# Other durations in the planner's table of a two-block transformer kernel on one core

## The chip, the cores and the metric

The kernel runs on one core of a Trainium2 chip. The metric is the device time of one execution in microseconds. A core has TensorE (PE, matrix products, with the loading of weights shown apart as PEld), VectorE (DVE), ScalarE (ACT), GpSimd (POOL) and SyncE (SP), which issues the loads. Every engine works through its own queue in order, and a semaphore makes an instruction wait for one on another engine.

## The reference

Two layers of a decoder block and then one block with a mixture of experts, for 256 tokens of 1024 features, all in float32.

```python
def first_block(x, mem, ...):
    h = x
    for l in range(DEPTH):                      # DEPTH = 2
        mix = hybrid_mixer(h, ...)              # recurrence and windowed attention, gated
        h = layer_norm(DEEPNORM_ALPHA * h + mix, ln1_g[l], ln1_b[l])
        h = layer_norm(DEEPNORM_ALPHA * h + cross_attention(h, mem, ...), ln2_g[l], ln2_b[l])
        h = layer_norm(DEEPNORM_ALPHA * h + swiglu(h, ffn_wi[l], ffn_wo[l]), ln3_g[l], ln3_b[l])
    return h
```

The second block modulates its input by vectors that come from a condition (`silu(cond) @ w + b`), attends to a neighbourhood on a grid and to a context, adds a gated spatial unit, and sends every token to two of four experts in one of four groups (16 experts, 512 hidden features each).

## The kernel before

*Products.* Weights come from memory in units of 128 x 1024 elements (512 KB). Each unit is split into two rounded parts: ACT writes `hi` (L425, in `_prep`), DVE writes `lo` = unit - `hi` (L426). A product is three matmuls, hi*hi, hi*lo and lo*hi (`mm3`, L540 to L542). With the weights stationary (`feat_block`) a unit is 24 matmuls of 256 columns, with the tokens stationary (`token_block`) it is 12 of 512 columns for the two token tiles of 128 tokens. Six pairs of `hi` and `lo` tiles exist, and a few units are split ahead (`prepare`, L489).

*Streams.* The work is written as generators ("streams"): parts of the recurrence, attention groups (`swa_group`, L957), norms (`layer_norm`, L662), products, and so on. A stream emits some instructions and yields the engines whose work it waits for, or a condition. `Streams.run` (L208) holds a list of streams in order of priority and decides which one goes on. It serves main streams and, behind them, fill streams that use the gaps. Products that can always run stand last, so they fill the time in which the chains of small steps wait.

*The planner.* `Net.record` (L289) runs the whole body once without emitting anything. In that dry run a `Clock` (L37) takes the place of the chip: `Clock.cost` (L75) gives the duration of each instruction, `Clock.issue` (L95) puts it on its engine's queue behind what it needs, with `HOP` for the way from one engine to another. The order found is kept as a script and the real run repeats it. Three decisions hang on the clock:

- In `Streams.run`, `clock.now` is the planned front of PE. The first stream in the list whose due time has passed goes on (L240); if none is due, the one that is due first (L238). After a step its due time is the end of the engines that it named, plus `HOP` (L256).
- In `Net.step` (L429) an additional weight split is planned when the dry run's vector and scalar engines both stand more than 1.0 us behind `clock.now` (L434).
- In `Net.weight` (L462) the products for the modulation's vectors (`ada`, L1311, its DVE products at L1328) advance by one unit, after at least 2 weight units if the planned vector engine stands behind `clock.now`, after 16 in any case (L476).

Where a unit is loaded to (`lender`, L399) follows from the order and from how many tiles are in use at each step of it.

The steps named below: in `layer_norm` the sum with the residual (L672, DVE), the square (L676, ACT, with a bias and a sum), small DVE steps (L680 to L686), the power on GpSimd (L687) and the last product (L691, DVE); transposes by PE (`flip`, L649); in `modulated` the scaling of the rows ahead of the transposes (L1372, ACT); in `router` (L1655) a copy of the shift (L1663, DVE) and eight products with it (L1667, PE); in `swa_group` the exponentials (L988, ACT); in `cross_q` a copy out of a bank (L1086, ACT), which the transposes behind it read.

Of the kernel before, what the change touches and what calls it, by code (L numbers as in the profile page):

```python
# [27 lines left out]
# columns of w_in  # L28
# [3 lines left out]
def f(ap):  # L32
    """The float32 pattern of an operand that was rounded for the tensor engine."""
    return ap.bitcast(F)


class Clock:  # L37
    """Stands for the chip in a dry run: what instructions take, each engine in its order, each after what it needs."""

    BASE, ROW, CELL, HOP = 1 << 40, 1 << 16, 128, 0.15  # L40
# [34 lines left out]
    def cost(engine, op, out, ins, accum):  # L75
        size = lambda a: int(np.prod([d[1] for d in tuple(a.ap)[1:]]))
        n = max([size(a) for a in [out] + ins if a is not None] or [1])
        if engine == "tensor":
            rhs = ins[1] if len(ins) > 1 else out
            n = size(rhs)  # L80
            if op == "transpose":
                return 2 * 128 / 2400.0
            part = tuple(out.ap)[0][1] / 128.0 if tuple(out.ap)[0][1] < 64 else 1.0
            slow = 4 if rhs.dtype != R or n < 256 else 1
            return max(part * n * slow / 2400.0, size(ins[0]) * (4 if rhs.dtype != R else 1) / 2400.0) + 0.0027
        if op == "dma_start":
            return n * 512 / 360e3
        if engine == "scalar":
            return 0.13 + n / 1300.0 + (0.09 if accum else 0.0)
# [3 lines left out]
        return 0.3 + 0.16 * n if op == "tensor_tensor" else 0.1  # L93

    def issue(self, engine, op, args, kw):  # L95
# [14 lines left out]
        hop = lambda w: w[0] + (self.HOP if w[1] != who else 0.0 if who == "tensor" else 0.06)  # L110
# [19 lines left out]
    def peak(self, tag, n):  # L130
        """How many tiles of that tag are in use at once, by the number of units taken."""
        count = [0] * (n + 1)
        for kind, first, last in self.lives.values():
            if kind == tag:
                for i in range(first, min(last, n) + 1):
                    count[i] += 1
        return count
# [16 lines left out]
class Shelf:  # L154
    """Tiles of a dry run."""
# [8 lines left out]
class Marks(dict):  # L164
    """What is there, and since when."""
# [19 lines left out]
class Late:  # L185
    """A stream that may go on in the next run."""
# [5 lines left out]
class Streams:  # L192
    """Runs several generators that emit instructions, in order of priority.

    A generator yields the engines whose work it waits for; a function is yielded to wait for its truth.
    The order is found in a dry run, by the clock, and repeated from script.
    """

# [9 lines left out]
    def run(self, main, fill=()):  # L208
        """Runs main to its end but for the streams in it that are Late; fill serves the gaps; what is left has to end the next time."""
# [54 lines left out]
class Net:  # L264
# [24 lines left out]
    def record(self, body, lend=True):  # L289
        """A dry run of body, for the order of its instructions and of its weights; then it can run."""  # L290
# [16 lines left out]
    def lasting(self, *tiles):  # L307
        """Tiles that are of use after the dry run's body."""
# [41 lines left out]
    def prepare_const(self):  # L350
        nc, c = self.nc, self.const
        # softplus(-lambda) of both layers, then its multiples
# [33 lines left out]
    def _consumed(self, back):  # L386
        """The raw unit is of no more use."""
# [7 lines left out]
    def _free(self, i):  # L395
        """The units before unit i that are not kept are of no more use."""
        self.splits = set(j for j in self.splits if j >= i or j in self.held)

    def lender(self):  # L399
        """Where the next unit may be loaded to; tiles are lent as long as none will be short of them."""  # L400
# [28 lines left out]
    def step(self):  # L429
        """After each step of a stream."""  # L430
# [20 lines left out]
    def keep(self, n):  # L451
        """Waits until n more units may be kept."""
# [4 lines left out]
    def drop(self, i):  # L457
        """Unit i has been kept and is of no more use."""
# [3 lines left out]
    def weight(self, src, cols=512, raw=False, kept=None):  # L462
        """The next unit, [128, 1024 / cols, cols]: (hi, lo), or as it is; kept: takes its number until it is dropped."""
# [25 lines left out]
    def prepare(self, i, taken=False):  # L489
        """Splits ahead of unit i, as far as the units held allow; taken: not that unit itself."""  # L490
# [12 lines left out]
    def _dry_prepare(self, i, end, taken):  # L503
        """What follows is not known yet and taken for units to be split."""
# [39 lines left out]
    def feat_block(self, x, src):  # L544
        """[feature, token] product: W stationary; src(k): unit of input chunks 2k and 2k + 1, x = (hi, lo) [128, 8, 256]."""
# [16 lines left out]
    def token_block(self, x, src, done=None, tmajor=False, ready=None):  # L562
        """[token, feature] product: x() stationary; done(t, bank) when a token tile is through; ready(t, q): x is there."""
# [44 lines left out]
    def split(self, hi, lo, src):  # L608
        """hi + lo = src exactly, each with the tensor engine's mantissa."""
# [36 lines left out]
    def flip(self, b, src, n=4):  # L646
        """Transposes n [128, 128] blocks of src into a bank."""
# [10 lines left out]
    def bcast(self, row_ap, n):  # L658
        """A DRAM row on every partition."""
        return bass.AP(tensor=row_ap.tensor, offset=row_ap.offset, ap=[[0, 128]] + list(row_ap.ap)[-n:])  # L660

    def layer_norm(self, t, h, res, gb, hn, after):  # L662
        """hn()[:, t] = LN(alpha h + res) with g, b; then after(t). The squares are taken about the mean of the first half."""
# [15 lines left out]
        # minus the mean; how far it is from the first half's  # L679
# [15 lines left out]
    def transposes(self, t, new):  # L695
        """The new h of token tile t transposed, as (hi, lo)."""
# [12 lines left out]
    def norms(self, l, i, h, res, new, after, early):  # L709
        """The streams that take the sums res into new["hn"] and after it; new[t]: that token tile is through."""  # L710
# [26 lines left out]
    def gelu2(self, out, x):  # L737
        """out = 2 gelu(x) for a bank x."""
# [8 lines left out]
    def rnn_conv(self, l, hT, st):  # L747
        """xc (feature, token) and its rounded parts."""
# [21 lines left out]
    def rnn_gates(self, l, st):  # L770
        """tanh of half the recurrence gate's and the input gate's argument."""
# [24 lines left out]
    def rnn_scan(self, l, st):  # L796
        """y = h gelu(gr) as (hi, lo)."""
# [5 lines left out]
        for k in range(8):  # L803
            # u = tanh(-log_a / 2)
# [5 lines left out]
        for h in range(2):  # L810
            i = (slice(None), slice(4 * h, 4 * h + 4), slice(None))
            s = self.k4().rearrange("p (k c) -> p k c", c=256)
            # a = (1 - u) / (1 + u), from the exponential by one correction
# [8 lines left out]
            # b = sqrt(1 - a^2) i xc, sqrt(1 - a^2) = sqrt(u) (1 + a)  # L822
# [39 lines left out]
    def tanh_gate(self, l, hT, col, st, name, wait=None):  # L862
        """tanh of half the gate's argument."""
# [22 lines left out]
    def swa_q(self, l, hT, st, n, ready=None):  # L886
        """Half the heads of q, scaled, rotated and transposed."""
# [29 lines left out]
    def swa_kv(self, l, hT, st):  # L917
        """k and v of both token tiles in a bank; then k, each head twice, rotated and transposed with zeros for the other half."""
# [38 lines left out]
    def swa_group(self, l, g, st):  # L957
        """Attention over the window with sinks, four heads."""
# [66 lines left out]
    def branches(self, l, st):  # L1025
        """(feature, token) sum of the gated branches as (hi, lo)."""
# [26 lines left out]
    def residual(self, x, w, res, ready=None, tmajor=(False, True)):  # L1053
        """x() @ w by token: banks res[n, t]."""
# [7 lines left out]
    def cross_k(self, l, c, st, away=False):  # L1062
        """Keys of the memory, two heads; away: out to the memory."""
# [16 lines left out]
    def cross_q(self, l, hT, st, old):  # L1080
        """Two heads by token, then two by feature."""
# [24 lines left out]
    def cross_heads(self, l, hp, st):  # L1106
        """Attention over the memory, two heads: (feature, token) as (hi, lo)."""
# [45 lines left out]
    def ffn(self, l, hT, res, old, first):  # L1153
        """The gated product: banks res[n, t]."""
# [61 lines left out]
    def first_hidden(self, t, first):  # L1216
        """The first hidden features of a token tile, found by token."""
# [1034 lines left out]
```

## Time and profile before

| | |
|---|---|
| median of 3 runs | 1573.4 us (1572.85 to 1573.48) |
| span of the profiled execution | 1570.5 us |
| PE busy | 1519.7 us (97%), 9434 instructions |
| DVE busy | 1183.8 us (75%) |
| ACT busy | 907.3 us (58%) |
| GpSimd busy | 42.1 us (3%) |
| read from memory | 339.71 MB, 218 GB/s over the span |

Busy time is the union of an engine's instructions. Matmuls are pipelined, so a record is longer than the distance between two starts; the distance is what PE needs for one. The granted clock is TensorE's, as a share of 2.4 GHz.

### The profile page before, as it was taken

To read this page: it belongs to the slowest core of one execution; us is meant where nothing else is said; L and a number is where in the kernel's file an instruction comes from. 1 tells how busy PE (TensorE), PEld (TensorE's weight loads), DVE (VectorE), ACT (ScalarE), POOL (GpSimd) and SP (SyncE) were. 2 spreads that over 40 slices of the span, in tenths; PEclk is the share of its full clock that TensorE was granted. 3 is DMA by queue.
4 is the path that set the end of the run, shared out by engine and by line. 5 is a ranking of instruction groups with operands and counts; after the bars stand their busy time and mean duration, and the time that the engine had idled before them with its cause. 6 is when DMAs were issued, how large, how long until landed. Compare 5 with 4: busy or idle time off the path is not lost. (4 is left out here: it accounts for less than half of the span.)

```text
span 1570.5 us, 24658 instructions
## 1 busy us (share of the span) xinstructions
PE 1519.7 (97%) x9434; PEld 1349.3 (86%) x9434; DVE 1183.8 (75%) x1715; ACT 907.3 (58%) x1350; POOL 42.1 (3%) x48
## 2 busy tenths in 40 slices
PE   8999999999999999999999999999899999999997
PEld 7998999887999979988988779999687778888886
DVE  6968877467887668778877577766675678999996
ACT  6687544444444445775556544444555568787774
POOL 0000000000000010000000000000020000000000
PEclk9999999999999999999999999999899989999999
DMA  9545647558766555346575487765463539999972
GB/s 350 165 136 177 238 150 270 188 185 287 244 217 209 183 201 161 114 156 208 195 282 179 128 297 244 240 205 165 138 235 121 162 130 316 391 375 391 380 280 82
DMA packets 188476, 344.55 MB, mean 219 GB/s; under 512 B 12352, under 2 KB 67520, under 8 KB 187456
## 3 DMA queue, kind: packets, MB, share of 16 engines
q1 hardware_dynamic: 187328, 339.76, 63.1%
q0 software_dynamic: 1024, 3.15, 0.6%
q8 instruction: 76, 1.25, 0.3%
q14 instruction: 48, 0.39, 0.1%
HBM read 339.71 MB, written 3.15 MB: 218 GB/s over the span
## 5 line engine op out<-in xcount | busy, mean ns | idle before, releaser
L540 PE MATMUL bank<-act,hi 128*128 128x256 f32 x1664 | 476.7, 286 | 0.0
L542 PE MATMUL bank<-act,lo 128*128 128x256 f32 x1664 | 470.8, 283 | 0.0
L541 PE MATMUL bank<-act,hi 128*128 128x256 f32 x1664 | 470.7, 283 | 0.0
L426 DVE TENSOR_TENSOR lo<-raw,hi 128x1024 fp32r<-128x1024 f32 x220 | 264.6, 1221 | 94.2 <-ACT hi L425 89.2
L540 PEld LDWEIGHTS bank<-act,hi 128*128 128x128 f32 x1664 | 319.0, 192 | 5.2 <-issue 3.6
L541 PEld LDWEIGHTS bank<-act,hi 128*128 128x128 f32 x1664 | 319.1, 192 | 2.1 <-issue 1.0
L542 PEld LDWEIGHTS bank<-act,lo 128*128 128x128 f32 x1664 | 318.9, 192 | 0.0
L540 PE MATMUL bank<-hi,act 128*128 128x512 f32 (+1 forms) x752 | 301.2, 401 | 7.9 <-ACT hi L425 6.2
L426 DVE TENSOR_TENSOR lo<-act,hi 128x1024 fp32r<-128x1024 f32 x222 | 264.2, 1221 | 50.6 <-ACT hi L425 49.3
L541 PE MATMUL bank<-lo,act 128*128 128x512 f32 (+1 forms) x752 | 294.0, 391 | 0.5 <-DVE lo L426 0.5
L542 PE MATMUL bank<-hi,act 128*128 128x512 f32 (+1 forms) x752 | 293.8, 391 | 0.0
L425 ACT ACTIVATE hi<-raw 128x1024 fp32r<-128x1024 f32 x220 | 228.5, 1055 | 103.4 <-PE bank L541 39.7
L425 ACT ACTIVATE hi<-act 128x1024 fp32r<-128x1024 f32 x222 | 227.8, 1054 | 78.6 <-PE bank L541 39.7
L426 DVE TENSOR_TENSOR lo<-k,hi 128x1024 fp32r<-128x1024 f32 x122 | 146.1, 1221 | 40.8 <-ACT hi L425 35.4
L540 PEld LDWEIGHTS bank<-hi,act 128*128 128x128 f32 x752 | 144.0, 192 | 37.7 <-ACT hi L425 7.9
L542 PEld LDWEIGHTS bank<-hi,act 128*128 128x128 f32 x752 | 144.0, 191 | 31.3 <-DVE act L611 1.5
L541 PEld LDWEIGHTS bank<-lo,act 128*128 128x128 f32 x752 | 144.4, 192 | 28.1 <-DVE lo L426 1.0
L425 ACT ACTIVATE hi<-k 128x1024 fp32r<-128x1024 f32 x122 | 126.5, 1055 | 37.8 <-PE bank L541 19.8
L540 PE MATMUL bank<-hi,k 128*128 128x512 f32 (+1 forms) x320 | 121.5, 380 | 0.0
L541 PE MATMUL bank<-lo,k 128*128 128x512 f32 (+1 forms) x320 | 121.5, 380 | 0.0
L542 PE MATMUL bank<-hi,k 128*128 128x512 f32 (+1 forms) x320 | 121.1, 378 | 0.0
L542 PEld LDWEIGHTS bank<-hi,k 128*128 128x128 f32 x320 | 60.1, 188 | 11.4
(281 smaller groups left out, 1514.7 us busy)
## 6 DMA issues: line engine op xcount, KB each, us to landing
act<-in_w_dram SPq DMA_DIRECT2D x90, 512.0 KB, 7.3
raw<-in_w_dram SPq DMA_DIRECT2D x58, 512.0 KB, 6.2
raw<-in_w_in_dram SPq DMA_DIRECT2D x57, 512.0 KB, 4.0
k<-in_w_dram SPq DMA_DIRECT2D x44, 512.0 KB, 7.9
act<-in_ffn_wi_dram SPq DMA_DIRECT2D x78, 256.0 KB, 6.1
act<-in_w_in_dram SPq DMA_DIRECT2D x32, 512.0 KB, 6.9
raw<-in_ffn_wi_dram SPq DMA_DIRECT2D x54, 256.0 KB, 4.2
act<-in_ffn_wo_dram SPq DMA_DIRECT2D x24, 512.0 KB, 6.4
```

Source lines behind the costliest of these rows:

```text
L425: self.nc.scalar.activation(hi, raw, AF.Copy)
L426: self.nc.vector.tensor_tensor(lo, raw, f(hi), op=OP.subtract)
L540: mm(out, lhs[0], rhs[0], start=start, stop=False)
L541: mm(out, lhs[0], rhs[1], start=False, stop=False)
L542: mm(out, lhs[1], rhs[0], start=False, stop=stop)
```

## The change

The constants of the planner's table change; `HOP` goes from 0.15 to 0.17 us and a new `DRAIN` of 0.28 us stands for the way from PE to another engine. All other lines of the diff take out comments and docstrings. Times in the table are microseconds, `n` is the number of elements in a row.

```diff
-    BASE, ROW, CELL, HOP = 1 << 40, 1 << 16, 128, 0.15
+    BASE, ROW, CELL, HOP, DRAIN = 1 << 40, 1 << 16, 128, 0.17, 0.28
...
             if op == "transpose":
-                return 2 * 128 / 2400.0
-            part = tuple(out.ap)[0][1] / 128.0 if tuple(out.ap)[0][1] < 64 else 1.0
-            slow = 4 if rhs.dtype != R or n < 256 else 1
-            return max(part * n * slow / 2400.0, size(ins[0]) * (4 if rhs.dtype != R else 1) / 2400.0) + 0.0027
+                return 0.109
+            if rhs.dtype == R:
+                return max(n, 256) / 2400.0 + 0.0135
+            half = any(tuple(a.ap)[0][1] <= 64 for a in (out, rhs))
+            return 2 * max(n / 1200.0 + 0.0025, 0.112) * (0.65 if half else 1.0)
         if op == "dma_start":
             return n * 512 / 360e3
         if engine == "scalar":
-            return 0.13 + n / 1300.0 + (0.09 if accum else 0.0)
+            few = sum(size(a) == 1 for a in ins) * 0.06 if n > 1 else 0.0
+            return 0.1 + few + n / 1200.0 + (0.1 if accum else 0.0)
...
-        return 0.3 + 0.16 * n if op == "tensor_tensor" else 0.1
+        return 0.4 + 0.16 * n if op == "tensor_tensor" else 0.1
...
-        hop = lambda w: w[0] + (self.HOP if w[1] != who else 0.0 if who == "tensor" else 0.06)
+        hop = lambda w: w[0] + ((self.DRAIN if w[1] == "tensor" else self.HOP) if w[1] != who else 0.0 if who == "tensor" else 0.06)
```

`few` counts operands of one element in a row, such as a bias; a sum that is written along counts too. The entries of the vector engine stay as they are.

## Rows read from the trace of the kernel before

**Rows 1.** The page, part 1: busy time, share of the span, instructions of each engine.
```profile
PE 1519.7 (97%) x9434; PEld 1349.3 (86%) x9434; DVE 1183.8 (75%) x1715; ACT 907.3 (58%) x1350; POOL 42.1 (3%) x48
```

**Rows 2.** Stages: stretch, its length, busy time of each engine, clock, DMA share.
```profile
core 0: us, PE busy (x) PEld busy (x) DVE busy (x) ACT busy (x) POOL busy (x), PEclk, DMA share, GB/s
...
136.00:145.00 9.00, 6.72 (x55) 4.77 (x54) 7.50 (x10) 6.18 (x16) 0.00 (x0) 1.00 0.45 124
...
704.00:715.00 11.00, 7.95 (x58) 5.79 (x57) 8.27 (x10) 7.75 (x20) 0.00 (x0) 0.84 0.42 127
...
1256.00:1275.00 19.00, 15.42 (x73) 12.75 (x73) 14.84 (x47) 9.65 (x21) 2.21 (x4) 0.73 0.41 138
1275.00:1420.00 145.00, 145.00 (x688) 120.95 (x687) 132.60 (x140) 118.56 (x145) 0.00 (x0) 1.00 0.91 328
```

**Rows 3.** Waits of PE: who for whom, us in total, times, longest.
```profile
PE bank L649 <- ACT k L1372: 6.3, 2, 4.7
...
PE bank L649 <- DVE small L680: 5.4, 2, 2.9
```

**Rows 4.** PE's timeline at the router: start, us, instruction, idle time before and releaser.
```profile
1115.28 1.93 PE L1667 MATMUL bank<-c2t,k 128*128 128x20 f32 x16 [1.52 <-DVE k L1663]
1117.06 0.48 PE L540 MATMUL bank<-hi,act 128*128 128x512 f32 x1
...
1117.86 0.63 PE L540 MATMUL bank<-hi,act 128*128 128x512 f32 x1
...
1120.85 0.57 PE L541 MATMUL bank<-lo,act 128*128 128x512 f32 x1
```

**Rows 5.** PE's timeline in two undisturbed places, and a wait behind the second.
```profile
129.80 0.28 PE L542 MATMUL bank<-act,lo 128*128 128x256 f32 x1
129.92 0.28 PE L540 MATMUL bank<-act,hi 128*128 128x256 f32 x1
...
281.16 0.39 PE L541 MATMUL bank<-lo,act 128*128 128x512 f32 x1
281.39 0.39 PE L542 MATMUL bank<-hi,act 128*128 128x512 f32 x1
282.46 0.66 PE L649 MATMUL bank<-ident,k 128*128 128x128 f32 x4 [0.69 <-ACT k L1086]
```

**Rows 6.** The page, part 5: costliest groups, count, busy us, mean ns, idle before.
```profile
L540 PE MATMUL bank<-act,hi 128*128 128x256 f32 x1664 | 476.7, 286 | 0.0
...
L540 PE MATMUL bank<-hi,act 128*128 128x512 f32 (+1 forms) x752 | 301.2, 401 | 7.9 <-ACT hi L425 6.2
...
L540 PE MATMUL bank<-hi,k 128*128 128x512 f32 (+1 forms) x320 | 121.5, 380 | 0.0
```

**Rows 7.** ACT's timeline ahead of the router.
```profile
1111.26 0.72 ACT L676 ACTIVATE k<-k,small 128x512 f32<-128x512 f32 x1 [1.96 <-DVE k L672]
...
1111.98 1.05 ACT L425 ACTIVATE hi<-k 128x1024 fp32r<-128x1024 f32 x1
1112.93 1.04 ACT L425 ACTIVATE hi<-raw 128x1024 fp32r<-128x1024 f32 x1
```

**Rows 8.** ACT's timeline: the copy that reads a bank of PE.
```profile
281.81 0.60 ACT L1086 ACTIVATE k<-bank 128x512 f32<-128x512 f32 x1 [3.00 <-PE bank L542]
```

**Rows 9.** One line, L687: count, shortest, median and longest in ns, first and last start.
```profile
L687 POOL TENSOR_TENSOR small<-small,half x12: 547/990/1930, 255.8 to 1125.1; 128x1 f32<-128x1 f32 x12
```

**Rows 10.** DVE's timeline in a norm: a split between two small steps.
```profile
357.27 1.23 DVE L426 TENSOR_TENSOR lo<-raw,hi 128x1024 fp32r<-128x1024 f32 x1
358.41 0.21 DVE L686 TENSOR_SCALAR small<-small 128x1 f32<-128x1 f32 x1
```

**Rows 11.** DVE's timeline: products of the modulation ahead of a norm.
```profile
903.13 1.54 DVE L1328 SCALAR_TENSOR_TENSOR k<-k,cz,k 128x512 f32<-128x512 f32 x2
904.58 0.68 DVE L672 SCALAR_TENSOR_TENSOR k<-act,bank 128x512 f32<-128x512 f32 x1
```

**Rows 12.** One line, L425: what ended ACT's idle time before it, us, times.
```profile
  PE bank L541: 99.2, 58
```

## The prediction

> **What bounds the kernel now.** I read the page first: TensorE (PE) is busy 1519.7 us, 97% of the span of 1570.5 us [rows 1]. All that another order of the same instructions can win is the 50.8 us in which it is not. Next I cut the span into stretches [rows 2]: a row gives the length and PE's busy time, and the difference is PE's idle time there. Eight short stretches, each the end of a phase, hold 31.2 us of it: 136 to 145 (the first of them, 2.28 us), 355 to 368, 566 to 579, 704 to 715 (3.05 us), 905 to 918, 1112 to 1136, 1198 to 1232 and 1256 to 1275 (the last, 3.58 us). The other 19.6 us are nearly all the start, before the first weights are there, and the last sum with its stores, which this change does not touch. Between the stretches PE is full; in the experts' part it is busy 145.00 of 145.00 us, though DVE works 132.60 us of it and the DMA engines 0.91 of the time.
>
> Last I read what PE waited for [rows 3]. The reader is to see that the waits are few and each has its own chain: the small steps of a norm (L680, up to 2.9 us), the scaling ahead of the transposes of the second block's input (L1372, up to 4.7 us).
>
> There is a second loss at these places: the granted clock is 0.84 and 0.73 in two of them, and 1.00 in the experts' part [rows 2]. Behind the router's wait, 512-column matmuls from 1117.86 to 1120.85 are seven intervals in 2.99 us [rows 4], 0.43 us each, the pace of 1.2 GHz; elsewhere they start 0.23 us apart [rows 5], the pace of 2.4 GHz. Seven fast ones take 1.59 us, so this slow stretch costs 1.4 us.
>
> **The change, part by part.** No instruction is added or removed. The table steers the dry run, and through it three things: which stream emits next (one is ready when PE's planned front has passed its due time), the additional weight splits (allowed when the planned DVE and ACT stand 1.0 us behind PE), and the places of the modulation's weight units (allowed when the planned DVE stands behind PE). So an entry has no price of its own: it moves the order, and the order moves the 50.8 us.
>
> *PE.* A rounded matmul of 256 columns goes from 256/2400 + 0.0027 = 0.1094 us to 0.1202, one of 512 from 0.2160 to 0.2268. The starts stand 0.12 us and 0.23 us apart [rows 5], so the new values are the chip's at its high clock. There are 3 x (1664 + 752 + 320) = 8208 of them, three lines of each kind [rows 6]; the planned PE becomes 8208 x 0.0108 = 88.6 us longer. This is the large edit. The old plan believed that PE does 5 to 10% more between two steps of a chain than it does, and put that much more of it there than was needed.
>
> *ACT.* A split of 1024 columns goes from 0.918 to 0.953 us; two in a row start 0.95 us apart [rows 7]. A square with a bias and a sum (L676) goes from 0.614 to 0.747 us; the next instruction starts 0.72 us after it [rows 7]. The 256-column exponentials of attention (L988) go from 0.417 to 0.533 us by the same formula. So chains over ACT become longer in the plan too, which takes back part of what the slower PE gives.
>
> *The way from PE to a reader.* It goes from 0.15 to 0.28 us, other crossings from 0.15 to 0.17. The matmul that starts at 281.39 is over, by the new entry, at 281.62 [rows 5], and the ACT copy that reads its bank starts at 281.81 [rows 8], 0.19 us later. The old entry is 0.04 us too short and the new one 0.09 too long: an error of the same order in the other direction.
>
> *What stays wrong.* GpSimd's power in a norm (L687) gets 0.56 instead of 0.46 us; the median of its twelve records is 0.99 us [rows 9]. Even if part of a record lies beside the next step, the plan stays some 0.4 us early in each norm. And no entry knows the slow clock.
>
> Now the waits that an order can move. The router's matmul (L1667) held PE for 1.52 us until L1663 was through, while the matmuls of the next unit, which ran right behind it from 1117.06, stood queued after it [rows 4]; one such unit is 12 x 0.227 = 2.72 us of work. Put first, it covers the wait: 1.5 us, and 2.9 us if the slow stretch of 1.4 us goes with it. L1663 came late because two norm chains and splits stand before it, with squares of 0.72 us [rows 7] that the old table had at 0.61. Bounds nothing and 2.9 us; I take 1.5.
>
> For that choice the Trainium skill has a rule: the page "TensorE: Matmul & The Clock Gate", section "Why this matters for your kernels", warns that an idle gap between bursts of matmuls brings the clock back to half. The trace shows the clock down here, after 1.52 us of idle time and 1.9 us of 20-column matmuls. By the rule, closing the gap would give back both, 2.9 us instead of 1.5, and the time would be 1.4 us lower than my sum.
>
> The ends of the two attention phases (136 to 145 and 704 to 715, 2.28 + 3.05 = 5.3 us) are chains that finish after the matmuls of the gates, which fill between their steps, have run out. With PE at its real pace the chains, which go first, are served after 5 to 10% fewer of those, and some are left for the end; the longer ACT entries work against it. Bounds nothing and 5.3 us; I take half, 2.7.
>
> In the norm chains at 355, 566, 905 and 1112 a weight split of DVE stands between L684 and L686: it starts at 357.27 and L686 1.14 us later [rows 10]; the other three look the same. These splits feed the matmuls that fill the gap, so the forecast counts nothing for them. If the new order has them ahead of the chain, the bound is 4 x 1.14 = 4.6 us.
>
> I count nothing for the 0.69 us wait at 282.46 [rows 5] and its kind: the stream is offered as soon as its mark is set, before the copy that it needs is priced. Nor for the 4.7 us behind L1372 [rows 3], where nothing else may run yet.
>
> Sum: 1.5 + 2.7 = 4.2 us. The profiled execution's span of 1570.5 us is 2.9 us under the median of 1573.4, and I keep that difference: 1570.5 - 4.2 + 2.9 = 1569.2 us.
>
> **The rivals.** *The waits stay (no change).* For it: most of the eight stretches are chains with too little to fill them, and no table makes more of it. The errors that remain (0.09 us too long from PE, 0.4 too short on GpSimd) are as large as those removed, and ACT's longer entries cancel PE's. Against it: the 8208 matmuls are the bulk of the plan, so the order will hardly come out the same. Nothing gained and nothing lost is 1573.4 us; with the router's wait or one attention end more or less it lies between 1570.3 and 1576.5. That the order does not change at all, so that the change does nothing, belongs here.
>
> *Weight work lands ahead of the chains (slower).* PE's plan grows and DVE's entries stay, so DVE's planned lead grows by 24 x 0.0108 = 0.26 us with each unit of 24 matmuls. Both conditions hold earlier, more splits are queued early, and the modulation's products (L1328) are drawn together. DVE works in order: what is queued ahead of a norm's first step delays the chain, and PE with it. The trace has a case: two such products start at 903.13 and L672, a norm's first step, follows at 904.58, 1.45 us later [rows 11]. A unit for both conditions has four, 2.9 us. Against it: splits wait mostly for PE to free a buffer (99.2 us behind L541 alone [rows 12]), so buffers, more than this rule, set their time. It decides from two chains on: 2 x 2.9 = 5.8 us, 1579.2 us; one chain alone stays within what can be measured.
>
> **How the numbers follow.** A measurement of this kernel can tell about 0.2%, 3.1 us, from no change: faster is under 1570.3 us, slower over 1576.5. The gain as summed gets 0.42 (1569.2 us, its own range 1562 to 1570.3), the waits that stay 0.32, weight work ahead of the chains 0.26. The likeliest gives 1569.2 us. The range reaches down by most of the upper bounds, 2.9 + 5.3 + 4.6 = 12.8 us, of which I take 11.4 since they hardly all come, and up by two chains and one slow stretch behind them, 5.8 + 1.4 = 7.2 us: 1562 to 1580.6. Beyond its ends I leave 2 in 10.
>
> **What would show it.** The counts and PE's spacing stay. Forecast right: the idle time of the two attention ends falls from 5.3 towards 2.7 us, and L1667 no longer waits 1.5 us. No change: the ends of the phases still hold about 31 us. Slower: L426 or L1328 stands right ahead of L672, or between it and L691, in more places than before, with longer waits of L649 behind. The prediction would be wrong altogether if PE became idle inside the experts' part, where it has no idle time now: with DMA at 0.91 and DVE at 132.60 of 145 us, an order that loads later would show there, as waits of L540 for L425.

## The result and the profile after

The changed kernel takes 1590.3 us against 1573.1 us, a ratio of 1.0105 with a 95% interval of 1.0093 to 1.0117: it is 17 us slower. The forecast was 1569.2 us, in a range of 1562.0 to 1580.6 us.

The profiled execution has a span of 1586.7 us, 16.2 us more than before. First the page, part 1, of the changed kernel, which answers to [rows 1]:

```profile
PE 1524.4 (96%) x9434; PEld 1353.1 (85%) x9434; DVE 1185.1 (75%) x1715; ACT 907.0 (57%) x1350; POOL 42.3 (3%) x48
```

The counts are the same. PE is idle for 62.3 us instead of 50.8 (span less busy time): 11.5 of the 16.2 us. The other 4.7 us are longer busy time of the same instructions. Most of it is slow clock: the mean granted clock is 0.982 instead of 0.984, some 3.4 us of the span. Lines of the changed kernel are those of before plus 2 (L540 is L542).

Part 5 of the page answers to the first row of [rows 6]: PE's commonest matmul, which had no idle time before it, now has 6.8 us, and one instruction of ACT ended nearly all of that.

```profile
L542 PE MATMUL bank<-act,hi 128*128 128x256 f32 x1664 | 478.0, 287 | 6.8 <-ACT act L612 6.7
```

PE's waits (who for whom, us in total, times, longest) answer to [rows 3]:

```profile
PE bank L542 <- ACT act L612: 9.4, 4, 6.7
PE bank L651 <- DVE k L1403: 7.4, 3, 2.9
...
PE bank L1004 <- DVE k L996: 5.8, 6, 2.1
PE bank L651 <- DVE act L693: 4.0, 2, 2.5
PE bank L651 <- DVE small L682: 3.5, 2, 2.6
...
PE bank L1669 <- DVE k L1665: 1.5, 1, 1.5
...
PE bank L651 <- ACT k L1374: 1.3, 1, 1.3
```

The longest wait is new. L996 is the scaling in attention, L1665 the router's, whose wait of 1.5 us is still there. L1403, a scaling ahead of transposes in the second block (L1401 of before), held PE for 0.3 us in before, and L1374 (L1372 of before) for 6.3 us in two waits [rows 3]. In stretches (columns as in [rows 2]):

```profile
60.00:110.00 50.00, 47.72 (x365) 44.63 (x364) 36.21 (x85) 32.38 (x82) 0.00 (x0) 1.00 0.37 125
110.00:155.00 45.00, 41.07 (x314) 35.30 (x313) 38.49 (x74) 36.87 (x80) 0.00 (x0) 1.00 0.50 166
...
197.00:205.00 8.00, 1.29 (x9) 0.98 (x7) 1.99 (x3) 0.99 (x2) 0.00 (x0) 0.83 0.82 274
205.00:213.00 8.00, 7.86 (x51) 7.67 (x51) 6.93 (x8) 6.29 (x9) 0.00 (x0) 0.75 0.42 146
...
690.00:735.00 45.00, 41.83 (x322) 36.10 (x321) 32.83 (x68) 34.58 (x76) 0.00 (x0) 1.00 0.49 169
...
920.00:935.00 15.00, 9.00 (x41) 7.32 (x40) 13.60 (x30) 6.53 (x10) 3.92 (x3) 0.77 1.06 365
...
1290.00:1435.00 145.00, 145.00 (x686) 120.91 (x685) 131.70 (x139) 119.20 (x146) 0.00 (x0) 1.00 0.88 324
```

One stretch stands out: from 197 to 205 us PE does 1.29 us of work in 8. Elsewhere the losses are small: 2.28 us in 60 to 110, where before had none, and 7.10 us in the two stretches with an attention end (110 to 155, 690 to 735), where before had 5.33. So of the 11.5 us of idle time 6.7 are the one wait, 2.3 the stretch from 60 to 110 and 1.8 the attention ends; all other places, some better and some worse, add 0.7. The experts' part is still full.

What PE waits for near 204 us is on ACT's timeline (start, us, instruction, count, idle time before and releaser):

```profile
193.02 1.09 ACT L873 ACTIVATE act<-bank 128x512 f32<-128x512 f32 x2
...
195.88 1.06 ACT L427 ACTIVATE hi<-act 128x1024 fp32r<-128x1024 f32 x1
203.93 2.84 ACT L612 ACTIVATE act<-act 128x512 fp32r<-128x512 f32 x4 [6.98 <-DMA act<-in_memT_dram]
206.67 1.04 ACT L427 ACTIVATE hi<-act 128x1024 fp32r<-128x1024 f32 x1
207.62 1.06 ACT L873 ACTIVATE act<-bank 128x512 f32<-128x512 f32 x2
```

L612 here are the four splits of memT, the memory that the cross attention reads. L873 is the tanh of the recurrence's gate, whose last two instructions stand behind them. The branches' product needs that gate and can't be offered before it. ACT waits 6.98 us for memT's data, and so does everything behind. SP issued the loads only at 198.09 us; from 185 to 206 us it waited three times, 7.6 us in all, for DVE to be through with a unit (L428) before it could load another into that place, and memT's loads stood behind:

```profile
197.47 0.53 SPq L335 DMA_DIRECT2D raw<-in_w_out_dram  x1
198.09 1.96 SPq L335 DMA_DIRECT2D act<-in_memT_dram  x4
```

PE meanwhile has nothing but the product of the memory itself:

```profile
204.61 0.58 PE L542 MATMUL bank<-act,hi 128*128 128x256 f32 x1 [6.71 <-ACT act L612]
205.34 0.58 PE L543 MATMUL bank<-act,hi 128*128 128x256 f32 x1
...
208.70 0.41 PE L543 MATMUL bank<-act,hi 128*128 128x256 f32 x1
208.91 0.35 PE L544 MATMUL bank<-act,lo 128*128 128x256 f32 x1
209.10 0.28 PE L542 MATMUL bank<-act,hi 128*128 128x256 f32 x1
209.22 0.28 PE L543 MATMUL bank<-act,hi 128*128 128x256 f32 x1
```

After the first two the starts stand 0.21 us apart, the pace of 1.2 GHz, and from 209.10 on 0.12: the first 18 of these matmuls take 4.49 us instead of some 2.2. The place costs 6.7 + 2.3 = 9.0 us.

In the kernel before, the order was the other one. ACT's timeline of it, then SP's:

```profile
191.95 0.60 ACT L871 ACTIVATE act<-bank 128x512 f32<-128x512 f32 x1 [0.84 <-PE bank L542]
193.62 3.14 ACT L610 ACTIVATE act<-act 128x1024 fp32r<-128x1024 f32 x5 [1.07 <-DVE act L841]
```

```profile
183.68 2.00 SPq L333 DMA_DIRECT2D act<-in_memT_dram  x4
```

The gate's tanh came first. The row of five is the split of the recurrence's output and behind it the four of memT, whose loads were issued 10 us before.

### The profile page after: what moved, and what is told of

Same layout as the page of the kernel before. It is cut to its first block, busy times and chain, and to the rows that moved or that the text cites. A ratio compares the mean times of both kernels' runs of the same rounds, so it can differ in the third digit from the quotient of the medians.

```text
span 1586.7 us, 24674 instructions
## 1 busy us (share of the span) xinstructions
PE 1524.4 (96%) x9434; PEld 1353.1 (85%) x9434; DVE 1185.1 (75%) x1715; ACT 907.0 (57%) x1350; POOL 42.3 (3%) x48
## 5 line engine op out<-in xcount | busy, mean ns | idle before, releaser
L542 PE MATMUL bank<-act,hi 128*128 128x256 f32 x1664 | 478.0, 287 | 6.8 <-ACT act L612 6.7
L428 DVE TENSOR_TENSOR lo<-raw,hi 128x1024 fp32r<-128x1024 f32 x221 | 267.2, 1221 | 107.6 <-ACT hi L427 105.9
L542 PEld LDWEIGHTS bank<-act,hi 128*128 128x128 f32 x1664 | 319.7, 192 | 13.4 <-ACT act L612 6.9
L428 DVE TENSOR_TENSOR lo<-act,hi 128x1024 fp32r<-128x1024 f32 x226 | 270.9, 1221 | 72.9 <-ACT hi L427 69.4
L542 PE MATMUL bank<-hi,act 128*128 128x512 f32 (+1 forms) x752 | 301.7, 401 | 8.9 <-ACT hi L427 6.2
L427 ACT ACTIVATE hi<-act 128x1024 fp32r<-128x1024 f32 x226 | 232.7, 1054 | 82.6 <-PE bank L543 47.3
L542 PEld LDWEIGHTS bank<-hi,act 128*128 128x128 f32 x752 | 144.5, 192 | 36.8 <-ACT hi L427 6.2
L428 DVE TENSOR_TENSOR lo<-k,hi 128x1024 fp32r<-128x1024 f32 x117 | 140.0, 1220 | 35.7 <-ACT hi L427 35.1
L427 ACT ACTIVATE hi<-k 128x1024 fp32r<-128x1024 f32 x117 | 121.3, 1057 | 53.9 <-PE bank L543 22.7
L542 PE MATMUL bank<-hi,k 128*128 128x512 f32 (+1 forms) x320 | 121.5, 380 | 0.0
L543 PEld LDWEIGHTS bank<-lo,k 128*128 128x128 f32 x320 | 60.2, 188 | 11.3 <-DVE lo L428 0.7
```

Of the source, the lines that this page charges most:

```text
L427: self.nc.scalar.activation(hi, raw, AF.Copy)
L428: self.nc.vector.tensor_tensor(lo, raw, f(hi), op=OP.subtract)
L542: mm(out, lhs[0], rhs[0], start=start, stop=False)
L543: mm(out, lhs[0], rhs[1], start=False, stop=False)
```

## The experiments

The theory after this reading: with PE's planned time longer, a step of the memory (`memory_in`, which loads memT and emits its splits at once) passes the recurrence's last gate, and that is most of the loss. The rivals were the attention ends, other tables' entries, and the mere draw of another order. In the table, "attention idle" is PE's idle time in 110 to 155 and 690 to 735 us, 90 us less PE's busy time in the two rows. The times are medians. The ratio compares a run with executions of before that were taken beside it and is not the quotient of two medians; for e5, whose executions spread from 1574.4 to 1580.4 us, the two differ most (1.0022 and 1.0012).

| run | us | ratio, 95% interval | attention idle, us |
|---|---|---|---|
| before | 1573.1 to 1574.1 | | 5.33 |
| after | 1590.3 | 1.0105 [1.0093, 1.0117] | 7.10 |
| e1 after, memory behind the gate | 1580.2 | 1.0040 [1.0026, 1.0055] | 6.08 |
| e2 PE's entries alone | 1587.0 | 1.0082 [1.0065, 1.0099] | 3.89 |
| e3 all but PE's | 1584.2 | 1.0061 [1.0044, 1.0078] | 13.05 |
| e4 all but the ways | 1580.8 | 1.0045 [1.0031, 1.0060] | 2.36 |
| e5 a way of 0.16 | 1575.3 | 1.0022 [1.0011, 1.0032] | 6.52 |
| e6 a way of 0.14 | 1582.1 | 1.0054 [1.0038, 1.0071] | 6.91 |
| e7 ACT's entries alone | 1583.4 | 1.0066 [1.0049, 1.0083] | 12.62 |
| e8 e4, memory behind the gate | 1582.5 | 1.0055 [1.0039, 1.0072] | 2.36 |
| e9 after, memT on its own queue | 1581.3 | 1.0046 [1.0029, 1.0063] | 6.65 |
| e10 e2, memory behind the gate | 1578.1 | 1.0027 [1.0017, 1.0038] | 3.89 |
| e11 all but ACT's, memory behind the gate | 1571.6 | 0.9987 [0.9977, 0.9996] | 2.26 |
| e12 the ways alone | 1574.9 | 1.0005 [0.9995, 1.0015] | 8.68 |
| e13 e1, ACT's surcharge halved | 1573.6 | 0.9996 [0.9986, 1.0005] | 3.04 |
| e14 e1, no surcharge | 1567.6 | 0.9957 [0.9941, 0.9974] | 3.89 |
| e15 e11, ACT's fixed part 0.14 | 1563.6 | 0.9934 [0.9918, 0.9951] | 2.79 |

### The memory's place

**e1** makes the memory wait for the gate, in the changed kernel:

```diff
-            yield lambda: "rnn" in st and "free" in st
+            yield lambda: "rnn" in st and "free" in st and "gg" in st
```

> The new table, and the stream that loads and splits the memory (memory_in) waits for one more mark, the finished recurrence gate (gg); nothing else differs. Theory: in the changed kernel the memory's four ACT splits stand ahead of the gate's last tanh in ACT's queue and wait for their load, so the branch product and PE wait (6.7 us idle, and 20 matmuls that take 4.5 instead of 2.4 us behind it, 8.8 us together). With the gate first that wait goes: 1590.3 - 8.8 = 1581.5 us, 1578 to 1584. Rival (the loss is spread over all the chains, since every one is served in another order, and this wait is only where it shows): 1587 or more.

It took 1580.2 us, 10 us less. In the trace memT is no earlier: ACT waits for it still, but with the gate ahead of it.

```profile
198.84 1.08 ACT L873 ACTIVATE act<-bank 128x512 f32<-128x512 f32 x2
203.18 2.80 ACT L612 ACTIVATE act<-act 128x512 fp32r<-128x512 f32 x4 [3.26 <-DMA act<-in_memT_dram]
```

Its stretches:

```profile
197.00:205.00 8.00, 8.00 (x69) 8.00 (x68) 4.89 (x6) 4.52 (x8) 0.00 (x0) 1.00 0.63 214
205.00:213.00 8.00, 8.00 (x69) 8.00 (x69) 7.56 (x9) 4.72 (x6) 0.00 (x0) 1.00 0.41 144
```

PE is busy in all of both, where the changed kernel had 1.29 and 7.86 us. But e1 draws an order of its own. **e9** does not: the instructions of PE, DVE and ACT stand in the changed kernel's order, and only the four loads of memT in each layer are issued by GpSimd, whose queue is empty there.

```diff
-            self.load(t[:, s, :], v[:, s, :])
+            (self.nc.sync if between or self.dry else self.nc.gpsimd).dma_start(t[:, s, :], v[:, s, :])
```

> The changed kernel with every instruction of PE, DVE and ACT in the same place; the four loads of memT alone are issued by GpSimd, whose queue is empty there, and not by SP, where they stood behind a load of weights until 198.1 us. The order is not drawn again, so this separates the memory's late data from the draw. Theory: they start as soon as their tile is free (before 192 us), the splits do not hold up ACT for 7.0 us, the product's wait of 6.7 us falls under 2.5 us and the slow clock behind it goes: 1581 to 1586 us against 1590.3. Rival (the wait is only where the new order happens to lose what it would lose elsewhere, or the tile comes free late): 1588 us or more.

It took 1581.3 us, 9.0 less than the changed kernel (6.9 between the two profiled executions). GpSimd issued the loads at 174.95 us (first row), and ACT no longer waited for them (second fence):

```profile
174.95 3.04 POOL L634 DMA_DIRECT2D act<-in_memT_dram  x4 [173.25 <-DVE act L843]
```

```profile
196.52 1.06 ACT L427 ACTIVATE hi<-act 128x1024 fp32r<-128x1024 f32 x1
197.47 2.18 ACT L612 ACTIVATE act<-act 128x512 fp32r<-128x512 f32 x4
```

PE's wait for L612 and the stretch from 197 to 205 us are now these:

```profile
PE bank L542 <- ACT act L612: 2.7, 3, 1.7
```

```profile
197.00:205.00 8.00, 6.80 (x56) 6.60 (x56) 8.00 (x10) 7.41 (x11) 0.00 (x0) 1.00 0.79 259
```

The 9.4 us of the changed kernel have lost the wait of 6.7; PE's other long waits stayed (7.4 us for L1403, 4.0 for L693, 3.5 for L682). So 9 of the 17 us are this place. The two edits have nothing else in common: at this place it was enough to mend either the position or the lateness of the data. It is not always enough (e8, below).

### Which entries

**e2** is the old table with PE's entries new (the first part of the diff), **e3** the new table without that part, **e4** the new table without the second part, the ways:

```diff
-            part = tuple(out.ap)[0][1] / 128.0 if tuple(out.ap)[0][1] < 64 else 1.0
...
+            if rhs.dtype == R:
+                return max(n, 256) / 2400.0 + 0.0135
...
-        hop = lambda w: w[0] + (self.HOP if w[1] != who else 0.0 if who == "tensor" else 0.06)
+        hop = lambda w: w[0] + ((self.DRAIN if w[1] == "tensor" else self.HOP) if w[1] != who else 0.0 if who == "tensor" else 0.06)
```

> The old table with only TensorE's entries new. Theory: TensorE's entries alone turn the order at the memory's splits, here in both layers, so PE waits some 7 us behind ACT's splits twice: 1582 to 1600 us, slower than before by at least 9. Rival (the longer ways and ACT entries cause the loss): 1570 to 1577.

> The new table with TensorE's entries left as they were. Theory: the memory's splits stay behind the gate's tanh, and the time is that of before within a few us: 1569 to 1577. Rival (the ways and ACT entries cause the loss, or any change of order costs): 1579 to 1590.

> The new table with HOP left at 0.15 and no DRAIN. Theory: the order turns in the second layer instead of the first; one wait of about 7 us: 1578 to 1588. Rival (DRAIN, 0.09 us too long by the spacing in the trace, makes the order worse): 1570 to 1576.

e2 shows the memory's wait at the same place, 6.6 us near 202 us, and one of 2.4 us in the second layer, near 771, where the theory had some 7. It changes all of PE's entries at once, the transposes and the float32 products too (in the table one of 256 columns onto 64 rows goes from 0.43 to 0.28 us); which of them turned the order is not shown. e4's time lies in its theory's range, but the long wait in the second layer is not there (see e8). e3 missed what the theory expected: it has no such wait and is 10 us slower than before all the same. Its attention ends are idle for 13.05 us. So there was a second cause, in ACT's entries or the ways. **e7** is the old table with ACT's entries alone, **e12** with the ways alone:

```diff
-            return 0.13 + n / 1300.0 + (0.09 if accum else 0.0)
+            few = sum(size(a) == 1 for a in ins) * 0.06 if n > 1 else 0.0
+            return 0.1 + few + n / 1200.0 + (0.1 if accum else 0.0)
```

> The old table with only ACT's entries new (with the ways from PE and between engines as before). The new table without PE's entries took 1584.2 us, its two attention ends idle for 12.9 us instead of 5.3. Theory: ACT's longer exponentials and squares make the chains longer in the plan, so each step is offered after more of the gates' matmuls; the fill runs out earlier and the attention ends get worse: 1575 to 1583 us, idle time of the two ends 6 to 12 us. Rival (the ways alone do it, since the new table with the old ways had no waits at the first attention end): 1570 to 1576 us and ends at 3 to 6 us.

> The old table with only the ways new (0.17, from PE 0.28). ACT's entries alone took 1583.4 us and ACT's and the ways together 1584.2 us, with nearly the same waits at the attention ends. Theory: the ways add little, 1572 to 1578 us, attention ends at 3 to 7 us of idle time. Rival of the draw: 1578 to 1584 us.

e7 took 1583.4 us, 0.4 above its range, with 12.62 us of idle time at the attention ends; e12 took 1574.9, level with before, though its ends (8.68 us) are worse than its theory said. So ACT's entries carry e3's time. GpSimd's entry, 0.10 us longer for a power, is new in e3 and e4 too and was not varied alone. PE's waits in e7, by totals (its lines are those of before plus 1):

```profile
PE bank L1003 <- DVE k L995: 7.1, 2, 3.5
...
PE bank L1011 <- ACT k L1005: 4.8, 4, 1.2
```

They are the transposes and the product of attention's last heads. The step comes late: the scores of the two last groups of heads (L978 of before) start at 124.55 and 127.13 us in before and at 127.23 and 133.67 in e7, while the gates' matmuls run out at 136.2 and 137.0 us. Behind the last of those scores before has 60 of the gates' matmuls left, e7 only 12: the others were spent between earlier steps. The start of the last group's scores, in before and in e7:

```profile
127.13 1.88 PE L978 MATMUL bank<-k,act 128*128 128x512 f32 x4
```

```profile
133.67 1.88 PE L979 MATMUL bank<-k,act 128*128 128x512 f32 x4
```

The column of idle time puts the parts together. PE's entries alone make the ends better (3.89 us against 5.33), ACT's alone (12.62) and the ways alone (8.68), which make the chains longer in the plan, make them worse; with PE's, either of them does no harm (2.36 in e4; 2.26 in e11 below), and both together do, against those two (7.10 in the change, 6.08 in e1). Against before the last two say little: moves without meaning give 6.52 and 6.91 (e5, e6). And the ends are not the whole: e4 has good ones and took 1580.8 us.

### The draw

The order is not a smooth function of the table. **e5** and **e6** move the old way by 0.01 us, which means nothing:

```diff
-    BASE, ROW, CELL, HOP = 1 << 40, 1 << 16, 128, 0.15
+    BASE, ROW, CELL, HOP = 1 << 40, 1 << 16, 128, 0.16
```

> The old table, with only the way between engines moved from 0.15 to 0.16 us, an amount without meaning. On PE more than half of the queue stands in another place. Theory of named causes (the time is lost where a particular step is put behind a late one: the memory's splits ahead of the gate, attention chains served later): neither is there, so 1570 to 1577 us, attention ends with 3 to 7 us of PE's idle time. Rival (the order of before is a lucky draw, and any other draw costs what the four changed tables cost, 0.4 to 0.9%): 1579 to 1588 us, the loss spread over many waits.

> The old table, with the way between engines at 0.14 instead of 0.15 us: the same question from the other side. Named causes: 1570 to 1577 us. Rival of the lucky draw: 1579 to 1588 us. If one of the two small moves costs nothing and the other several us, the draw matters, but before is not the only good one.

They took 1.8 and 8.6 us more than before: one held the theory's range, the other the rival's. Where e6 loses its 8.6 us is not shown. So a difference of a few us between two tables is no evidence for any one entry; only the ones that a trace ties to a place are.

**e8** is e4 with e1's edit, and a miss.

> The new table with the old ways (1580.8 us), and the memory's step also waits until the recurrence's last gate has been issued. Theory: the wait of 2.3 us near 205 us and its slow clock go, 3 to 5 us: 1575.5 to 1578 us. Rival (a redrawn order has its own waits, whatever the cause removed): no lower than 1579 us, with new waits elsewhere.

It took 1582.5 us (its profiled execution 1589.0, so its trace says where, not how much). In e4's first layer the memory stood behind the gate already; what PE waited for there (2.27 us at 204.79) was a weight split of ACT that stood behind memT's, whose data was late there too, and in e8 it still does (3.3 us). In e4's second layer the order had turned, as its theory said. ACT's timeline of that place, then the stretch:

```profile
767.13 0.63 ACT L612 ACTIVATE act<-act 128x512 fp32r<-128x512 f32 x1 [5.00 <-DMA act<-in_memT_dram]
...
771.42 1.07 ACT L873 ACTIVATE act<-bank 128x512 f32<-128x512 f32 x2
```

```profile
763.00:771.00 8.00, 8.00 (x69) 8.00 (x68) 3.24 (x5) 2.96 (x5) 0.00 (x0) 1.00 0.88 316
```

ACT waits 5.00 us for memT with the gate's last tanh behind it, but PE has other work for all of that time. So the position alone has no price, and with late data the right position did not save PE in the first layer. The edit removed no wait of PE and drew another order. **e10** gives the same edit to e2, where the memory was ahead of the gate in both layers:

> Only PE's entries new (1587.0 us), and the memory's step also waits until the recurrence's last gate has been issued. In that kernel the memory stood ahead of the gate in both layers (waits of 6.6 us near 202 us and 2.4 us near 771 us, with slow clock). Theory: both go, 1573 to 1579 us. Rival of the draw: any new order costs 2 to 9 us against before for other reasons as well, so 1579 to 1583 us with new waits elsewhere.

It took 1578.1 us, 9 less than e2, as the theory said. **e11** leaves out both causes, ACT's entries and the memory's place:

> The new table without ACT's entries, and the memory's step behind the gate: the two causes found so far taken out together. Theory: attention ends under 5 us of idle time, no wait near 200 us, 1570 to 1577 us, so at least level with before. Rival of the draw: 1577 to 1583 us, the loss in other places.

1571.6 us: level with before, 8.6 us below e1, from which only ACT's entries differ. That is as much as e6's move without meaning, so the time alone would not show it.

### The surcharge on ACT

**e13** and **e14** take e1 and lower the 0.06 us for each operand of one element to 0.03 and to nothing; **e15** takes e11 and moves ACT's fixed part from 0.13 to 0.14 us.

```diff
-            few = sum(size(a) == 1 for a in ins) * 0.06 if n > 1 else 0.0
+            few = sum(size(a) == 1 for a in ins) * 0.03 if n > 1 else 0.0
...
-            return 0.13 + n / 1300.0 + (0.09 if accum else 0.0)
+            return 0.14 + n / 1300.0 + (0.09 if accum else 0.0)
```

> The new table with the memory behind the gate (1580.2 us), and ACT's surcharge for each operand of one element at 0.03 instead of 0.06 us. An exponential of 256 columns is then 0.473 us in the table (starts stand 0.49 apart in the trace of before), a square 0.687: nearer to the chip than both tables. Theory (ACT's longer entries make the attention chains late, in proportion): between the two known ends, 1571.6 with the old entries and 1580.2 with the new: 1573 to 1579 us, attention ends idle less than the 6.6 us of the second. Rival of accuracy (the nearer to the chip, the better): 1571.6 us or less. Rival of the draw: anywhere, 1572 to 1583, with no relation to the attention ends.

> The same without the surcharge: an exponential of 256 columns is 0.413 us in the table, as in the old one (0.417), a square 0.627 (0.614), a split of 1024 columns stays at the new 0.953. Theory (the chains' own entries, not the splits', put the attention steps late): 1570 to 1575 us, attention ends idle under 3 us. Rival (the splits' entries do it): 1578 to 1583 us and ends as with the full surcharge.

> The kernel of 1571.6 us (new table, ACT's entries old, memory behind the gate) with ACT's fixed part moved from 0.13 to 0.14 us, an amount without meaning. If its level is owed to the two causes that it leaves out, it stays at 1570 to 1576 us; if it was a good draw, it goes to 1577 to 1583 us.

With the surcharge at 0.06, 0.03 and 0 the times are 1580.2, 1573.6 and 1567.6 us, in order, below the expected range at the last one. So, if the draw is left aside, the loss comes with the entries of the chains' instructions and not with those of the splits, which are the new ones in all three. The rival of accuracy is not borne out: for the exponentials 0.03 is nearest to the chip, and 0 is faster. (For the square 0.687 and 0.747 are about equally far from the 0.72 of [rows 7], unlike what was expected above.) Attention idle falls from 6.08 to 3.04 and 3.89 us, the last above the 3 that was expected; what remains in e14 are waits for weight splits. But e15, a move without meaning, took 8.0 us off e11 and fell below both of its ranges. That is more than a step of the surcharge, so part of the order of the three may be the draw, and these runs don't settle it.

e15 beats both kernels, at 0.9934 of before. Its page, part 1:

```profile
PE 1515.6 (97%) x9434; PEld 1348.8 (86%) x9434; DVE 1184.1 (76%) x1715; ACT 907.4 (58%) x1350; POOL 43.0 (3%) x48
```

PE's idle time is 1561.9 - 1515.6 = 46.3 us, 4.5 under before, and its busy time 4.1 us shorter, at a mean granted clock of 0.987 against 0.984. The four kernels with PE's entries and the ways new, the memory behind the gate and ACT's chains lighter than in the change (e11, e13, e14, e15) lie 0.5 to 10.4 us under the runs of before beside them; the three small moves of the old table (e5, e6, e12) lie 1.2 to 8.6 us over. How much of that is the table and how much the choice of four draws stays open.

## Why the prediction was wrong

**What bounds the kernel** held. The counts and PE's spacing stayed, PE's idle time (11.5 us) and its longer busy time (4.7 us), most of that slow clock, carry the whole difference, and the experts' part stayed at 145.00 of 145.00 us.

**PE's entries: the mechanism was right, and followed to one place only.** The prediction said that with PE at its real pace the chains are served after fewer matmuls of the gates, and booked that as a gain of 2.7 us at the attention ends [rows 2]. Without ACT's new entries the ends do so: 3.89 us in e10, all of it waits for weight splits, and 2.26 in e11 instead of 5.33. But that the chains, "which go first", are served earlier holds for every stream that stands before the gates, and `memory_in` is one. It was not looked at and stood in the sum at nothing. Served earlier, it put four splits into ACT's queue ahead of the gate, at a time when their data was not there. This is the step that failed, and it is 9 of the 17 us. PE's entries do it alone (e2) and without them it does not come (e3), but whether it comes in the first layer hangs on the rest of the table too (e4). The prediction priced only the rounded matmuls among PE's entries.

**ACT's entries: the sign was right, the size was not.** The prediction had them take back part of PE's gain. In the change, with the ways, they took more than all: the ends went from 5.33 to 7.10 us where 2.7 were to be saved. Between e1 and e11, which differ in ACT's entries, lie 8.6 us, 3.8 of them idle time of the ends (6.08 less 2.26); alone they cost 10 (e7). The slow clock behind the waits and the draw are in both, so how much of the other 8 us is theirs stays open. An exponential of 256 columns had 0.417 us and has 0.533; the chip needs 0.49, as ACT's timeline of before shows by its starts:

```profile
136.73 0.50 ACT L988 ACTIVATE k<-k,small 128x256 f32<-128x256 f32 x1
...
137.22 0.50 ACT L988 ACTIVATE k<-k,small 128x256 f32<-128x256 f32 x1
```

The entry that was too short served the chain sooner, as the starts of the scores in e7 show, and in these kernels that was the better order.

**The way from PE** was called an error of the same order in the other direction and had no term in the sum. For the ways alone that held: e12 is 1.0005 of before, though its attention ends are worse by 3.4 us. In the change it did not hold: without the ways (e4) it takes 1580.8 us, 9.5 less (the draw included), and the memory's order turns in the second layer only, where PE does not wait.

**The router's wait** of 1.5 us was to go. It is 1.53 us in the changed kernel as in [rows 4], and 2.9 us in e10, e11 and e15: the next unit's matmuls still stand behind L1669. It was assumed that the order would put them first; nothing in the rows said so. The table does move this wait, but not by that: it is 0.5 us in e3, e7 and e12 and 2.9 in e6, a move without meaning.

```profile
1129.88 2.88 PE L1669 MATMUL bank<-c2t,k 128*128 128x20 f32 x16 [1.53 <-DVE k L1665]
1132.59 0.77 PE L542 MATMUL bank<-hi,act 128*128 128x512 f32 x1
1133.16 0.63 PE L543 MATMUL bank<-lo,act 128*128 128x512 f32 x1
1133.59 0.63 PE L544 MATMUL bank<-hi,act 128*128 128x512 f32 x1
```

The starts behind it are again 0.43 us apart, half the clock, as in [rows 4].

**The norms** were bounded by 4.6 us of gain. In 920 to 935 us PE is idle for 6.00 us, with L651 waiting for L1403 as well; the same place in before, 905 to 920 us, has 3.76. The sum had no loss there. The 4.7 us behind L1372 [rows 3] were counted at nothing because nothing else could run there; that reading was wrong, since L1374 holds PE for 1.3 us in the changed kernel. Most of that gain was lost again beside it, to L1403 and to splits.

**The rivals.** "Weight work lands ahead of the chains" had the right sign and kind, work queued in order ahead of a step that PE needs, but on DVE, at the norms, and with a price of 5.8 us. What came was ACT, at a gate, with a load behind it. "The waits stay" was wrong in that they grew. The range ended at two chains and one slow stretch; a late load, which holds an engine's queue for as long as the load takes, was in no bound, though [rows 2] show the DMA engines at 0.4 to 0.9.

## What to carry to other kernels

When a planner's table changes, list every stream that the longer or shorter engine moves, with the in-order queue that it enters and whether its data will have landed by then; one that waits for a load must not stand ahead of a step that feeds the bound engine. An instruction that depends on a transfer should be emitted later than the transfer, or the transfer sooner on a free queue: here that alone was worth 9 us. What such a wait costs hangs on the other work of the bound engine: with the same order in e4's second layer PE did not wait. And measure what a table change without meaning does before a few us are read as the merit of an entry: here it was -8.0, +1.8 and +8.6 us.

## What was not expected of the hardware

The clock fell behind a wait much shorter than 1.5 us. In e12 the router's wait is 0.55 us:

```profile
1118.62 1.93 PE L1667 MATMUL bank<-c2t,k 128*128 128x20 f32 x16 [0.55 <-DVE k L1663]
1120.39 0.48 PE L540 MATMUL bank<-hi,act 128*128 128x512 f32 x1
...
1121.71 0.63 PE L542 MATMUL bank<-hi,act 128*128 128x512 f32 x1
1122.14 0.63 PE L540 MATMUL bank<-hi,act 128*128 128x512 f32 x1
```

The 512-column matmuls from 1121.71 on are 0.43 us apart all the same, and the granted clock is 0.57 in 1121 to 1125 us, after 1.00 in 1117 to 1121. What PE did before the fall was 0.55 us of idle time, 1.77 us of 20-column matmuls (1118.62 to 1120.39) and then 512-column ones up to 1121.7, at first 0.23 us apart. So the branch of the prediction that gave the clock back with the gap (2.9 instead of 1.5 us) would not have held with the gap nearly closed; no run here has it closed wholly. That branch went by the Trainium skill, "TensorE: Matmul & The Clock Gate", section "Why this matters for your kernels", which warns of idle gaps between bursts of matmuls; in this trace the clock falls with a gap of 0.55 us, and 20-column matmuls stand beside it.

The eight loads of memT, four in each layer, landed 6.0 us after their issue by SP in the median (4.3 to 6.5), in the changed kernel, and 3.9 us (3.2 to 8.3) after their issue by GpSimd in e9, which took 3.04 us to issue four against SP's 1.96. Why is not shown: they were issued at other times, beside other loads.
